# RMSNorm and matmul on one core: the loads of x move to ScalarE's DMA queue, in pieces of eight tiles

## The chip, the core and the metric

The kernel runs on one core of one Trainium2 chip. TensorE (PE), VectorE (DVE), ScalarE (ACT), GpSimd (POOL) and SyncE (SP) each run their own instruction list in order and wait for one another by semaphores. Transfers between HBM and the on-chip memory are issued by an engine (here SP, and ACT for one small one) and carried out by the core's 16 DMA engines. The metric is the device time of the core in microseconds (us), the median of several runs.

## The reference

```python
# x [16, 1024, 512] f32, gamma [512] f32, weight [512, 768] f32, eps
rms = np.sqrt(np.mean(x ** 2, axis=-1, keepdims=True) + eps)
x_norm = x / rms * gamma
return np.matmul(x_norm, weight).astype(np.float32)     # [16, 1024, 768]
```

## The kernel before

The 16,384 rows of x are 128 tiles of 128 rows. A tile of x is 256 KB of float32, a tile of the output 384 KB. Tiles go in pairs j = 0 to 63 (tiles 2j and 2j+1).

**The work on a tile.** gamma is folded into the weight once, at the start, and 1/rms is applied at the end, when the product leaves PSUM. So a tile goes through these steps: its rows are loaded into `xt` (line 176); ACT squares them and sums along the row (`square`, line 195); POOL casts them to bf16 (`cast`, line 187); PE transposes them as pairs of bf16 packed in a float32 word (`transpose_word`, line 229), and DVE copies the transposed tile back (`evac`, line 238); PE multiplies it by the weight in 8 matmuls (line 299) into one of three accumulators; ACT (even tiles, line 278) or DVE (odd tiles, line 280) scales the accumulator by 1/rms into `ot`; SP stores it (line 292). The last four tiles of every 16, from tile 16 on, are transposed by DVE in 32x32 blocks (line 270) after a POOL cast into `xq` (line 259).

**Buffers.** `xt` has two slots of 16 tiles, so tile i+32 overwrites tile i and may be loaded only when tile i has been cast and squared. `ot` has three slots of 8 tiles, so tile i+24 may be scaled only when the store of tile i's group has landed. PSUM has three accumulators, so tile i+3 may begin on PE only when tile i has been scaled.

**The order.** The class `Order` writes down every operation with what it reads and writes, in program order, and turns that into waits: each engine runs its own operations in the order written, and a transfer is issued by its engine at the place where it was written down. The main loop runs over the pairs. In the turn of pair j it writes down the casts, then the squares of the pair or pairs in `norm_turns` (pair j+4 for most of the run), then the matmuls of tiles 2j and 2j+1 with the transposes of pair j+2 between them, then the two scalings and the store, if the tile ends a group.

**The loads of x before the change.** All go out on SP, in the same list as the stores. Tiles 0 to 31 are loaded ahead of the loop, in pieces of 2, 2, 4, 8, 8 and 8 tiles, the first one before the two weight loads and the rest behind them. From there on, the loop calls

```python
        load_until((2 * j + AHEAD + XG - 1) // XG * XG)     # AHEAD = 20, XG = 16
```

at the head of each turn: groups of 16 tiles, as one load (tiles 32 to 79) or as two of 8 (from tile 80). SP issues in order, so a load that stands behind a store in SP's list is issued when that store's tiles have been scaled, and its data move behind that store's data. `rows` lays the tiles over the rows of x and out so that the bytes of one load or store lie together in each partition's stretch: a piece of 8 tiles is 16 KB of x, or 24 KB of the output, for each of 128 partitions.

Of the kernel before, what the change touches and what calls it, by code (L numbers as in the profile page):

```python
# [100 lines left out]
def kernel(  # L101
# [9 lines left out]
    PE, DVE, ACT, POOL, SP = nc.tensor, nc.vector, nc.scalar, nc.gpsimd, nc.sync  # L111
    order = Order(tc)
# [4 lines left out]
    x = x.flatten_outer_dims()  # L117
    out = out.flatten_outer_dims()
# [3 lines left out]
    NT = N // P  # L122
    NP = NT // 2
    XG, OG = 16, 8
    AHEAD = 20

    def stretches(group, parts):
        first, size, i = {}, {}, 0
        for g in range(NT // group):
            for n in parts.get(g, [group]):  # L130
                for t in range(i, i + n):
                    first[t], size[t] = i, n
                i += n
        return first, size

    last = NT // OG - 1
    x_first, x_size = stretches(XG, {0: [2, 2, 4, 8], **{g: [8, 8] for g in (1, 5, 6, 7)}})
    o_first, o_size = stretches(OG, {0: [1, 1, 2, 4], last - 1: [4, 4], last: [4, 2, 2]})

    def rows(ap, i, n):  # L140
        base, t = (x_first[i], x_size[i]) if i < XG else (i - i % XG, XG) if i < 2 * XG else (i - i % (2 * XG), 2 * XG)
        return ap[base * P:(base + t) * P, :].rearrange("(p t) d -> p t d", t=t)[:, i - base:i - base + n, :]

    def sb(name, shape, dtype):
# [26 lines left out]
    def x_of(i, n=1):  # L171
        return xt[i // XG % 2][:, i % XG:i % XG + n, :], cells("x", i // XG % 2, i % XG, n)

    def load(i):
        dst, to = x_of(i, x_size[i])
        order.transfer(SP, lambda: SP.dma_start(out=dst, in_=rows(x, i, x_size[i])), writes=to)  # L176

    starts = [i for i in range(NT) if x_first[i] == i]

    def load_until(i):  # L180
        while starts and starts[0] < i:
            load(starts.pop(0))

    def cast(i, n=1):
        src, of = x_of(i, n)
        s = i // 8 % 2
        run(POOL, lambda: POOL.tensor_copy(out=xb[s][:, i % 8:i % 8 + n, :], in_=src), of, cells("xb", s, i % 8, n))  # L187
# [3 lines left out]
    def square(i):  # L191
        src, of = x_of(i)
        j = squares[0] % 2
        squares[0] += 1
        run(ACT, lambda: ACT.activation(out=jk[j], in_=src[:, 0, :], func=AF.Square, accum_out=ssq[:, i:i + 1]),  # L195
            of, [("jk", j), ("ssq", i)])

    def root(i, n):
        s = slice(i, i + n)
        run(ACT, lambda: ACT.activation(out=rms[:, s], in_=ssq[:, s], func=AF.Sqrt, scale=1.0 / D, bias=eps_sb),  # L200
            [("ssq", t) for t in range(i, i + n)] + ["eps"], [("rms", i)])
        run(DVE, lambda: DVE.reciprocal(out=rstd[:, s], in_=rms[:, s]), [("rms", i)],  # L202
            [("rstd", t) for t in range(i, i + n)])

    def norms(i, n):
        for t in range(n):
            square(i + t)
        root(i, n)
# [6 lines left out]
    def norms_of_group(j):  # L215
        square(2 * j)
        square(2 * j + 1)
        if j in norm_end:
            root(*norm_end[j])
# [33 lines left out]
    def quad_of(j):  # L253
        return j // 2 if (2 * j) % XG >= XG - 4 and 2 * j >= XG else None

    def cast_quad(q):
        src, of = x_of(4 * q, 4)
        s = 4 * q // XG % 2
        run(POOL, lambda: POOL.tensor_copy(out=xq[s], in_=src), of, [("xq", s)])  # L259
        for t in range(4):  # L260
            xT_of[4 * q + t] = (xTq[s][:, t], ("xTq", s))
        words = xq[s].rearrange("p t d -> p (t d)").bitcast(F32).rearrange("p (a w) -> p a w", w=P)
        turned = xTq[s].rearrange("p t h m c -> p (t h m c)").bitcast(F32).rearrange("p (a m) -> p a m", m=P)
        for tokens in range(0, P, B):
            for features in range(0, P, B):
                quad_moves.append((turned[features:features + B, :, tokens:tokens + B],
                                   words[tokens:tokens + B, :, features:features + B], s))
# [4 lines left out]
    def move_quad(n):  # L272
        for _ in range(min(n, len(quad_moves))):
            move(*quad_moves.pop(0))
# [9 lines left out]
    def accumulator():  # L284
        return next(turns) % 3

    def store(i):
        first, n = o_first[i], o_size[i]
        s = first // OG % 3
        if i == first + n - 1:  # L290
            src = ot[s][:, first % OG:first % OG + n, :]
            order.transfer(SP, lambda: SP.dma_start(out=rows(out, first, n), in_=src), reads=cells("ot", s, first % OG, n))  # L292
# [12 lines left out]
    def matmuls(i, a, ks, feed=None):  # L305
        block, cell = xT_of[i]
        for k in ks:
            lhsT = block[:, k // 2, :, k % 2]
            hold(lhsT, cell)
            for half, lo, hi in ((0, 0, WIDE), (1, WIDE, O)):  # L310
                product(ops[a][:, lo:hi], lhsT, w_bf[:, k, lo:hi], k == 0, k == K - 1,
                        [cell, ("w", k, half)], [("ops", a, half)])
            if feed:
                feed()

    def finish_tile(i, a, engine):
        s = i // OG % 3

        before = [("ot", s, i % OG - 1)] if i == o_first[i] + o_size[i] - 1 else []
        scale(engine, ot[s][:, i % OG, :], ops[a][:, :O], rstd[:, i:i + 1],  # L320
              [("ops", a, 0), ("ops", a, 1), ("rstd", i)] + before, [("ot", s, i % OG)])
        store(i)

    def feeder(pairs, gaps, alone=False):
        queue = [(j, t, h) for j in pairs for t in range(2) for h in range(2)]
        calls = iter(gaps)

        def feed():
            for _ in range(next(calls)):
                j, t, h = queue.pop(0)  # L330
                transpose_word(j, t, h)
                if alone and h == 1:
                    evac(j, t, 1)
                elif (t, h) == (1, 1):
                    evac(j)
        return feed
# [6 lines left out]
    def load_weights(h):  # L343
        order.transfer(SP, lambda: SP.dma_start(out=w_f32[:, 2 * h:2 * h + 2, :].rearrange("p c o -> p (c o)"), in_=wv[:, h, :]),  # L344
                       writes=[("w_f", 2 * h), ("w_f", 2 * h + 1)])
# [1 line left out]
    load_until(2)  # L347
    load_weights(0)
    load_weights(1)
    load_until(2 * XG)  # L350

    run(DVE, lambda: DVE.memset(warm, 0.0), [], ["warm"])
    run(DVE, lambda: DVE.memset(eps_sb, float(eps)), [], ["eps"])  # L353
# [48 lines left out]
    mid, one, two, both = ([0, 0, 1, 1, 0, 1, 1, 0], [1, 1, 0, 1, 1, 0, 0, 0], [1, 0, 1, 0, 1, 0, 1, 0],  # L402
                           [1, 1, 1, 1, 1, 1, 1, 1])
    for j in range(1, NP):
        load_until((2 * j + AHEAD + XG - 1) // XG * XG)
        if j in (1, 2):
            cast(4 * j + 4, 4)
        elif j % 8 == 4 and j + 4 < NP:
            cast(2 * j + 8, 8)
        elif j % 8 == 6 and j + 2 < NP:  # L410
            cast(2 * j + 12, 4)
        if (2 * j + 2) % XG == 0 and 2 * j + 2 < NT:
            cast_quad((2 * j + 2 + XG - 4) // 4)
        elif 2 * j >= XG:
            move_quad(3)
        if j < 4:
            norms(2 * j + 2, 2)
        for pair in norm_turns.get(j, []):
            norms_of_group(pair)
        if j < 3:  # L420
            feed = feeder([j + 1], mid if j == 1 else one, alone=j == 1)
        elif j == 3:
            feed = feeder([4, 5], both)
        elif j + 2 < NP and quad_of(j + 2) is None:
            feed = feeder([j + 2], two)
        else:
            feed = None
        for i, engine in ((2 * j, ACT), (2 * j + 1, DVE)):
            a = accumulator()
            matmuls(i, a, range(K), feed)  # L430
            finish_tile(i, a, engine)
# [48 lines left out]
```

## Time and profile before

| what | value |
|---|---|
| runs | 208.95, 209.01, 209.52 us; median 209.01 us |
| the profiled execution's own time | 208.56 us |
| its span, first to last instruction | 206.8 us |
| PE busy | 192.9 us (93%) |
| DVE, ACT, POOL busy | 149.3, 144.5, 59.9 us |
| moved by DMA | 85.62 MB, mean 414 GB/s |
| read from and written to HBM | 35.13 MB and 50.33 MB |
| PE's last matmul ends | about 198.2 us |

The profiled execution took 1.8 us more than its span, and 0.45 us less than the median of the runs. Busy time is summed over the whole span and says little where two engines are near their limits at once; the rows by stretches of time say more. DMA shares are means over the 16 DMA engines.

### The profile page before, as it was taken

Reading aid. Unit: us, or ns where it says so; the run is one execution under the profiler, and the core shown is the slowest. Engines: PE = TensorE matmul, PEld = TensorE weight load, DVE = VectorE, ACT = ScalarE, POOL = GpSimd, SP = SyncE. Lnnn points to the kernel's source line nnn. Section 1 sums busy time; section 2 is a strip of 40 time slices with the busy share of each in tenths; the row PEclk is TensorE's granted clock in tenths of the full one; section 3 lists DMA queues with packets and bytes.
Section 4 is the critical chain, followed back from the end, with each engine's and each line's share of the span. In section 5 each row is a group of like instructions: output and inputs, shape, how many; then the busy total and the mean of one; then the engine's idle time right before and its main releaser. Section 6 shows DMA issues by size and latency. Waiting matters only on the chain.

```text
span 206.8 us, 2761 instructions
## 1 busy us (share of the span) xinstructions
PE 192.9 (93%) x1212; PEld 72.5 (35%) x717; DVE 149.3 (72%) x255; ACT 144.5 (70%) x343; POOL 59.9 (29%) x34
## 2 busy tenths in 40 slices
PE   7789999999999999998999999999999999999930
PEld 1234443432343333342333333433343333343300
DVE  0455647998589966998469984999569984999520
ACT  4798897868768496864977687677867787673310
POOL 2247651009300291004900660006700274000000
PEclk9999999999999999999999999999999999999996
DMA  6999999999999999999999999999999999999993
GB/s 225 423 445 428 387 385 444 456 396 428 428 445 425 417 426 455 425 409 433 431 415 436 428 445 403 439 417 447 418 441 414 437 433 441 418 442 409 414 415 141
DMA packets 5632, 85.62 MB, mean 414 GB/s; under 512 B 626, under 2 KB 628, under 8 KB 1780
## 3 DMA queue, kind: packets, MB, share of 16 engines
q1 hardware_dynamic: 5616, 85.46, 97.6%
q8 instruction: 7, 0.11, 0.2%
q14 instruction: 5, 0.04, 0.0%
q10 hardware_dynamic: 4, 0.00, 0.0%
HBM read 35.13 MB, written 50.33 MB: 413 GB/s over the span
## 4 chain that ended last, share of the span: by engine, by line
PE 71%; DMA 16%; DVE 5%; issue 2%; SPq 1%; ACT 1%; POOL 1%; ACTq 0%
PE ps L299 62%; DMA xt<-in_x_dram 16%; PE ps L229 8%; DVE ot L280 2%; DVE xTq L270 2%; DVE xT L238 1%; POOL xb L187 1%; ACT jk L195 0%; SPq L344 0%; SPq L176 0%; ACT ot L278 0%; SPq L292 0%; DVE rstd L202 0%; SPq L475 0%; ACTq L93 0%
## 5 line engine op out<-in xcount | busy, mean ns | idle before, releaser
L299 PE MATMUL ps<-w_bf,xT 128*128 128x256 bf16 (+1 forms) x783 | 144.9, 325 | 2.6 <-DVE w_bf L280 0.8
L278 ACT ACTIVATE ot<-ps,rstd 128x768 f32<-128x768 f32 x64 | 57.4, 897 | 42.3 <-PE ps L299 40.7
L195 ACT ACTIVATE jk<-xt 128x512 bf16<-128x512 f32 x128 | 78.8, 619 | 7.7 <-DMA xt<-in_x_dram 7.7
L187 POOL CAST xb<-xt 128x2048 bf16<-128x2048 f32 (+3 forms) x21 | 46.3, 2221 | 111.9 <-DMA xt<-in_x_dram 93.3
L280 DVE TENSOR_SCALAR ot<-ps,rstd 128x768 f32<-128x768 f32 x64 | 64.8, 1013 | 9.4 <-PE ps L299 8.7
L295 PEld LDWEIGHTS <-xT 128*128 128x128 bf16 x400 | 39.3, 98 | 60.2 <-issue 52.1
L229 PE MATMUL ps<-ident_f,xb 128*128 128x128 f32 x200 | 54.1, 274 | 0.9 <-POOL xb L187 0.9
L238 DVE COPY xT<-ps 128x1024 bf16<-128x1024 bf16 (+1 forms) x53 | 34.5, 653 | 24.0 <-PE ps L229 22.3
L270 DVE STREAM_TRANSPOSE xTq<-xq 32x256 f32<-32x256 f32 x112 | 48.7, 435 | 3.4
L229 PEld LDWEIGHTS ps<-ident_f,xb 128*128 128x128 f32 x200 | 28.2, 142 | 46.5 <-issue 42.7
L299 PE MATMUL ps<-w_bf,xTq 128*128 128x256 bf16 (+1 forms) x217 | 41.8, 324 | 0.4
L195 ACT ACTIVATION_READ_ACCUMULATOR jk<-xt 128x1 f32 x128 | 24.3, 190 | 0.0
L295 PEld LDWEIGHTS <-xTq 128*128 128x128 bf16 x112 | 11.0, 98 | 14.5 <-issue 14.5
L259 POOL CAST xq<-xt 128x2048 bf16<-128x2048 f32 x7 | 13.3, 1897 | 0.0
L202 DVE RECIPROCAL rstd<-rms 128x8 f32<-128x8 f32 (+3 forms) x20 | 3.9, 193 | 8.3 <-ACT rms L200 8.1
L200 ACT ACTIVATE rms<-ssq,eps_sb 128x8 f32<-128x8 f32 (+3 forms) x20 | 6.0, 300 | 0.7
L299 PE MATMUL ps<-warm 128*128 128x512 bf16 x10 | 4.4, 578 | 1.4 <-DVE eps_sb L353 1.4
L278 ACT ACTIVATE w_bf<-w_f,g_sb 128x768 bf16<-128x768 f32 x2 | 1.9, 936 | 1.1 <-DMA w_f<-in_weight_dram 1.1
L376 DVE COPY g_sb<-ps 128x4 f32<-128x4 f32 x1 | 0.2, 163 | 3.2 <-PE ps L370 3.2
L340 ACT ACT_TABLE_LOAD x1 | 1.3, 1283 | 1.5 <-SPq L434 1.5
L280 DVE TENSOR_SCALAR w_bf<-w_f,g_sb 128x512 bf16<-128x512 f32 (+2 forms) x3 | 1.4, 481 | 0.6 <-DMA w_f<-in_weight_dram 0.6
L370 PEld LDWEIGHTS ps<-ident_f,g_row 2*128 2x128 f32 x2 | 0.3, 202 | 2.6 <-issue 2.6
(10 smaller groups left out, 1.9 us busy)
## 6 DMA issues: line engine op xcount, KB each, us to landing
out_dram<-ot SPq DMA_DIRECT2D x13, 3072.0 KB, 16.5
xt<-in_x_dram SPq DMA_DIRECT2D x9, 2048.0 KB, 21.0
xt<-in_x_dram SPq DMA_DIRECT2D x3, 4096.0 KB, 22.7
out_dram<-ot SPq DMA_DIRECT2D x4, 1536.0 KB, 11.5
out_dram<-ot SPq DMA_DIRECT2D x3, 768.0 KB, 7.3
w_f<-in_weight_dram SPq DMA_DIRECT2D x2, 768.0 KB, 5.5
xt<-in_x_dram SPq DMA_DIRECT2D x2, 512.0 KB, 5.2
xt<-in_x_dram SPq DMA_DIRECT2D x1, 1024.0 KB, 9.0
```

Source lines behind the costliest of these rows:

```text
L187: run(POOL, lambda: POOL.tensor_copy(out=xb[s][:, i % 8:i % 8 + n, :], in_=src), of, cells("xb", s, i % 8, n))
L195: run(ACT, lambda: ACT.activation(out=jk[j], in_=src[:, 0, :], func=AF.Square, accum_out=ssq[:, i:i + 1]), of, [("jk", j), ("ssq", i)])
L200: run(ACT, lambda: ACT.activation(out=rms[:, s], in_=ssq[:, s], func=AF.Sqrt, scale=1.0 / D, bias=eps_sb), [("ssq", t) for t in range(i, i ...
L202: run(DVE, lambda: DVE.reciprocal(out=rstd[:, s], in_=rms[:, s]), [("rms", i)], [("rstd", t) for t in range(i, i + n)])
L229: run(PE, lambda: PE.transpose(out=tp[b][:, t, h, :], in_=words[:, lo:lo + P], identity=ident_f), cells("xb", s, j % 4 * 2 + t) + ["ident" ...
L238: run(DVE, lambda: DVE.tensor_copy(out=dst[:, t:t + n, :], in_=src[:, t:t + n, :]), [("tp", b)], cells("xT", j % 4, t, n))
L259: run(POOL, lambda: POOL.tensor_copy(out=xq[s], in_=src), of, [("xq", s)])
L270: run(DVE, lambda: DVE.transpose(out=dst, in_=src), [("xq", s)], [("xTq", s)])
L278: run(ACT, lambda: ACT.mul(out=dst, in_=src, mul=r), reads, writes)
L280: run(DVE, lambda: DVE.tensor_single_scalar(out=dst, in_=src, scalar=r, op=mybir.AluOpType.mult), reads, writes)
L295: run(PE, lambda: PE.ldweights(lhsT), [cell])
L299: run(PE, lambda: PE.add_instruction(mybir.InstMatmult(name=nc.get_next_instruction_name(), engine=mybir.EngineType.PE, ins=[PE.lower_ap(r ...
```

## The change

Three things are done. The pieces are 8 tiles throughout, so that tiles 32 to 79 are loaded in six pieces and not three. Loads of tiles 0 to 23 stay on SP ahead of the loop (`FIRST` = 24); all later loads are issued by ACT, so SP's list holds only stores from there on, and the first store stands right behind the load of tiles 16 to 23. And the places in the loop change: tiles 24 to 31 are loaded in the turn of pair 2, and from then on a piece of 8 in every fourth turn, beginning with tiles 32 to 39 in the turn of pair 5, each starting eleven pairs (`LEAD`) ahead. In ACT's list such a load stands behind the squares of its turn and ahead of the scaling of tile 2j. The layout of rows is the same as before for each tile. The instruction lists of PE, DVE and POOL are the same in both kernels; ACT's gains 13 DMA issues, and no wait; SP's loses 10 load issues.

```diff
-    AHEAD = 20
+    FIRST, LEAD = XG + OG, 11
...
-    x_first, x_size = stretches(XG, {0: [2, 2, 4, 8], **{g: [8, 8] for g in (1, 5, 6, 7)}})
+    x_first, x_size = stretches(OG, {0: [2, 2, 4]})
...
-        base, t = (x_first[i], x_size[i]) if i < XG else (i - i % XG, XG) if i < 2 * XG else (i - i % (2 * XG), 2 * XG)
+        base, t = (i - i % OG, OG) if OG <= i < XG else (x_first[i], x_size[i]) if i < OG else (i - i % XG, XG) if i < 2 * XG else (i - i % (2 * XG), 2 * XG)
...
         dst, to = x_of(i, x_size[i])
-        order.transfer(SP, lambda: SP.dma_start(out=dst, in_=rows(x, i, x_size[i])), writes=to)
+        queue = SP if i < FIRST else ACT
+        order.transfer(queue, lambda: queue.dma_start(out=dst, in_=rows(x, i, x_size[i])), writes=to)
...
-    load_until(2 * XG)
+    load_until(FIRST)
...
     for j in range(1, NP):
-        load_until((2 * j + AHEAD + XG - 1) // XG * XG)
...
         for pair in norm_turns.get(j, []):
             norms_of_group(pair)
+        if j == 2 or j > 2 and (j + LEAD) % 4 == 0:
+            load_until(2 * XG if j == 2 else 2 * (j + LEAD) + OG)
```

## The prediction

> **What bounds the kernel now.** I read the slices of the page first, then the queues, then busy time by stretches, then the waits and the timeline near a wait.
>
> ```profile
> PE   7789999999999999998999999999999999999930
> DMA  6999999999999999999999999999999999999993
> q1 hardware_dynamic: 5616, 85.46, 97.6%
> q8 instruction: 7, 0.11, 0.2%
> ```
>
> PE and the DMA engines are both full from the second slice to the end. q1 is SP's queue, with every load and store of the loop; q8 fetches instructions.
>
> ```profile
> 12.00:198.00 186.00, 183.71 (x1175) 69.92 (x694) 144.83 (x242) 137.12 (x329) 56.83 (x25) 1.00 1.00 426
> ...
> 21.00:24.00 3.00, 2.95 (x21) 1.26 (x13) 1.77 (x4) 2.31 (x7) 2.28 (x1) 1.00 1.01 421
> 24.00:27.00 3.00, 3.00 (x22) 1.22 (x12) 1.62 (x2) 3.00 (x10) 1.32 (x1) 1.00 0.93 287
> 42.00:45.00 3.00, 3.00 (x22) 1.18 (x13) 2.87 (x7) 2.08 (x6) 0.00 (x0) 1.00 0.94 374
> ...
> 198.00:201.00 3.00, 0.17 (x2) 0.00 (x0) 1.02 (x1) 0.00 (x0) 0.00 (x0) 1.00 0.97 406
> 201.00:204.00 3.00, 0.00 (x0) 0.00 (x0) 0.00 (x0) 0.00 (x0) 0.00 (x0) 0.89 0.72 299
> ```
>
> Columns: stretch, its length, busy PE, PEld, DVE, ACT, POOL, clock, DMA share, GB/s. The DMA share is 1.00 for 186 us at 426 GB/s: there is no gap to fill, in any stretch, only a rate. It drops at 24 to 27 (287) and at 42 to 45 (374). In the packet records of the trace a 16 KB packet takes 608 ns, a 24 KB one 912 and a 32 KB one 1,213, to the nanosecond, except in these stretches.
>
> How close is PE as a bound? The pairs repeat every 23.42 us for 16 tiles (SP's stores at 35.58 and 59.00). 16 tiles are 4.19 MB in and 6.29 MB out, so PE asks for 10.49 MB / 23.42 us = 448 GB/s. DMA gives 426. So DMA is the tighter of the two and a backlog grows.
>
> ```profile
> ACT jk L195 <- DMA xt<-in_x_dram: 7.7, 6, 3.0
> ...
> 95.65 0.63 ACT L195 ACTIVATE jk<-xt 128x512 bf16<-128x512 f32 x1 [3.03 <-DMA xt<-in_x_dram]
> 97.82 1.46 PE L299 MATMUL ps<-w_bf,xT 128*128 128x512 bf16 x8 [0.72 <-ACT ot L278]
> ```
>
> That backlog reaches PE once: tiles 64 to 79 come late, ACT's square waits 3.03 us, and PE 0.72. At the end, PE finishes at 198.2, DVE scales to 199.2, and the last store (768 KB) is issued at 199.5 and lands after 6.3, at 205.8. The first load finds an empty queue: 512 KB in 3.4 us, the least of all loads, of which 1.2 are data at 426. So 768 KB would take 1.8 + 2.2 = 4.0, and the end has some 2.3 us of backlog in it.
>
> **The change part by part.** I sum against the profiled span, 206.8; its execution took 208.56, 0.45 below the median.
>
> Bytes: the same. Packets: six pieces of 16 KB rows for three of 32 KB, 48 packets of 608 ns on each engine for 24 of 1,213, so +0.07 us.
>
> The slow stretches: (426 - 287) x 3 / 426 = 0.98 us, and (426 - 374) x 3 / 426 = 0.37. Both lie where all 16 engines finish a load with stores next. By the packet records the load packets there run long (850 to 1,190 ns for 608 at 24 to 27) and the stores do not; the later such places cost 0.15 us falling to 0.03, as the engines drift apart. From store to load nothing is lost. After the change the load of tiles 24 to 31 runs beside the first stores instead of ahead of them, so I count the 0.98 as gone. Bounds: 0, if it moves to wherever stores first start; -1.5, if all six places go. I take -1.0.
>
> Two queues on each engine: this is the cost that the trace doesn't show. Most of the time an engine now has load packets of one queue and store packets of the other before it. The 13 loads from ACT make 13 x 8 = 104 visits to the second queue on each engine. Bound above: the only second queue here, q8, needs 940 ns for its 16 KB packets (608 on q1), and the packet behind it is 360 to 470 long, so 0.34 + 0.36 = 0.7 us a visit, or 73 us. Bound below: on one queue, store to load costs 0, and load to store on engines that are out of step mostly 0. I take 0: q8's packets come alone to a sleeping queue, while here both are full, as the loads and stores are in the drifted stretches, which hold 426. A gain can't be excluded, but 426 against 431 (16 KB in 608 ns, 16 engines) leaves 2 us at most.
>
> The Trainium skill speaks against this change. "DMA: Bandwidth & Descriptors", "Rules for kernel authors", says that spreading transfers over queues brings no bandwidth, since they interleave on the same engines; the share of 1.00 agrees that there is none to be had. The same page, "Latency and other measured facts", gives copies over both queues 207 to 214 GB/s in each direction; as an estimate of mine, 414 in all would make 186 us at 426 some 5 us longer, and 428 one us shorter. No run here shows either.
>
> ACT's 13 issues: an issue of x takes SP 0.34 to 1.04 us, so 4.4 to 13.5 us of ACT's list. ACT waits 40.7 us for PE ahead of its scalings (L278), 0.92 in most pairs, and a scaling may be 1.6 us late (two tiles of 1.3 us on the other accumulators, less 0.90 for the scaling) before PE waits. So 0; without that cover, up to 13.5. The slots that the loads overwrite have been cast and squared several pairs earlier.
>
> The later loads: issued every 11.7 us; alternating with stores one takes 8 x (0.608 + 0.912) = 12.2 us, so the lag grows 0.5 a load, from 13.5 us to 19. The squares of these tiles come seven pairs after the issue, 20.5 us, with 1.6 of slack. They hold, and the 0.72 of PE goes. The margin at the last load is 3 us.
>
> The early loads: here the change costs something. By the GB/s of the stretches, the data of tile 23 end at 20.7 (cast at 21.72). Now ACT issues tiles 24 to 31 after its root at 15.9, data from about 17.4, and shares the engines with tiles 16 to 23, of which 3.2 us are left: they end at 23.8, are seen at 24.8, and the cast of 3.60 us ends at 28.4. PE's first transpose of tile 16 is at 28.31. PE waits 0.1 to 1.1 us; I take 0.3. Stores: the first start behind tile 23, 2 us earlier; their slots are due at 47.7, far away.
>
> PE's end is then 198.2 - 0.72 + 0.3 = 197.8, and with 2.3 us of backlog behind it a DMA saving of 1.0 reaches the end whole. Sum: 206.8 + 0.07 - 1.0 + 0 = 205.9 span, 207.65 execution, 208.1 in the median. Where this stall goes, the next to be late is again the data of the last stores.
>
> **The rivals.** *No change*, 209.0: the slow stretch comes back where stores start, and the total stays bytes over rate. For it: the share of 1.00. Against: nothing of the old hand-over is left.
>
> *All of it*, 206.1: six hand-overs gone (-1.5), and the engines, whose last packets end between 202.4 and 205.4 in the packet records, evener, so that no backlog is left: PE's end at 197.5, 1.3 to the last issue, 4.0 to land, 1.0 to the end, 203.8 of span. For it: it needs no more than the bounds above. Against: it needs a rate near 431 for 186 us.
>
> *Slower, by the switch between queues*: it cancels the gain at 1.0 us / 104 = 10 ns a visit and is slower by over 0.3% from 16 ns. At 50 ns, a small part of q8's 700 and about what a late hand-over costs, it is 5.2 - 1.0 = +4.2: 213.2. For it: every visit of q8 or q14 to an engine costs, and PE already asks for more than DMA gives. Against: both queues are never empty.
>
> That loads don't move to the second queue is excluded by the instruction lists.
>
> **How the numbers follow.** About 0.3% (0.63 us) is what a measurement of this kernel can tell from no change. Forecast 208.1, chance 0.35, own range 207.2 to 208.4. All of it, 0.10. No change, within 0.63, 0.15. Slower by the switch, 0.32; slower because PE waits early or ACT's issues run long (+1 to +2), 0.08. So faster 0.45, same 0.15, slower 0.40. The range reaches from the second case, less the 0.3% of a measurement, 205.5, to 50 ns a visit, 213.2; dearer switches are left out.
>
> **What would show it.** Right: 24 to 27 us above 400 GB/s, a second queue with about 27 MB, packets still at 608 and 912 ns, no wait of ACT near 95, PE's end near 197.8, DMA full to about 203. Wrong: load packets beside stores well over 608 ns and GB/s between 40 and 160 under 420; or PE waiting for the cast of tile 16 for over 2 us; or ACT's scalings waiting behind DMA issues.

## The result, and the profile after

The changed kernel takes 214.41 us in the median of 20 runs (209.17 to 219.45), the kernel before 209.0 us in 20 runs beside them (208.61 to 209.52): 2.6% slower, and above the predicted range, which ended at 213.2. The ratio is 1.0061, 95% interval [1.0038, 1.0084], if runs over 1.5% above a kernel's fastest are left out, as 13 of this kernel's 20 are; the kernel before has no such run, and the second and third profiles below show what goes with that scatter. Its profiled execution took 213.27 us, with a span of 211.4 at a mean granted TensorE clock of 0.996.

From the page of the changed kernel, the rows that answer to those of before (busy tenths in 40 slices; packets, MB and share of 16 engines for each queue):

```profile
PE   7789999999999999999999999999997989979890
DMA  6999999999999999999999999999999999887597
q1 hardware_dynamic: 4176, 58.20, 65.4%
q10 hardware_dynamic: 1876, 27.27, 30.7%
```

The second queue carries its 27 MB, as forecast. DMA, full up to the last slice before, now has holes in the last six. Busy time by stretches of the changed kernel, with the columns as before (stretch, length, PE, PEld, DVE, ACT, POOL, clock, DMA share, GB/s):

```profile
12.00:198.00 186.00, 180.63 (x1155) 67.84 (x673) 141.11 (x237) 135.16 (x327) 57.13 (x25) 1.00 0.98 413
...
24.00:27.00 3.00, 3.00 (x22) 1.18 (x13) 1.65 (x3) 3.00 (x8) 3.00 (x1) 1.00 0.98 310
42.00:45.00 3.00, 3.00 (x22) 1.22 (x12) 2.88 (x6) 2.12 (x5) 1.86 (x1) 1.00 1.02 437
...
189.00:192.00 3.00, 3.00 (x20) 1.22 (x12) 2.87 (x5) 0.90 (x1) 0.00 (x0) 1.00 0.38 164
195.00:198.00 3.00, 2.58 (x17) 0.69 (x8) 2.84 (x5) 0.90 (x1) 0.00 (x0) 1.00 0.23 94
```

The stretch at 24 to 27 us is slow still (310 for 287 GB/s, so 0.82 us is lost there for 0.98). At 42 to 45 the rate is back. Near 190 the loads are done, and PE is too late to give DMA stores: DMA works for 0.38 and 0.23 of the time. PE's last matmul ends at 205.9, 7.7 us later than before. What made PE late, from the waits of the changed kernel (us in total, times, longest):

```profile
DVE xTq L271 <- POOL xq L260: 10.2, 5, 3.2
...
ACT jk L196 <- DMA xt<-in_x_dram: 4.5, 5, 1.6
PE ps L300 <- DVE ot L281: 4.3, 6, 1.5
```

The first row is new: DVE's block transposes (the last four tiles of each 16) wait for POOL's cast of them. These casts, and not the squares, meet the late load first. One such place in the changed kernel's timeline (start, duration, engine, line; the idle time before it in brackets):

```profile
155.01 1.90 POOL L188 CAST xb<-xt 128x2048 bf16<-128x2048 f32 x1 [9.62 <-DMA xt<-in_x_dram]
156.85 1.90 POOL L260 CAST xq<-xt 128x2048 bf16<-128x2048 f32 x1
...
158.78 1.37 DVE L271 STREAM_TRANSPOSE xTq<-xq 32x256 f32<-32x256 f32 x3 [2.83 <-POOL xq L260]
...
161.85 0.48 PE L300 MATMUL ps<-w_bf,xT 128*128 128x512 bf16 x2 [1.15 <-DVE ot L281]
```

Read it downwards: the piece of tiles 104 to 111, issued at 131.57, is whole at 154.9. POOL casts four tiles for PE and then four for DVE, DVE starts 2.83 us late, its scaling of an odd tile behind that is late too, and PE waits 1.15 for the accumulator. Without the wait DVE would have begun at 155.95, so the piece was due at 155.95 - 3.74 = 152.2. On the median of the 16 engines it had landed at 150.1; the last engine came at 154.9. The squares of these tiles waited too, but only 0.92 us, from 154.05 on.

The packet records give a ledger. "Nominal" is all packets at their undisturbed times (611, 912 and 1,213 ns for 16, 24 and 32 KB, 460 for 12 KB), "excess" what they took above, "idle" the time without packets before and after 198 us, all in us per engine. "Spread" is the longest time between the first and the last of 16 engines in the landing of one transfer, "long stores" the 24 KB packets over 50 ns above nominal between 30 and 180 us. With the first packet at 2.0 us and up to 1 us of other queues' packets, which are left out here, a row adds up to the end of the data within 1.3 us, since neighbouring packets overlap a little. The profiled executions:

| kernel | us | nominal | excess | idle < 198 | idle > 198 | data end | PE end | spread | long stores |
|---|---|---|---|---|---|---|---|---|---|
| before | 208.56 | 199.0 | 2.4 | 0.2 | 1.9 | 205.4 | 198.2 | 3.8 | 14 |
| after | 213.27 | 199.2 | 3.4 | 5.0 | 0.8 | 210.1 | 205.9 | 9.1 | 128 |
| after, second (e9) | 209.65 | 199.2 | 3.0 | 2.1 | 0.4 | 206.4 | 202.1 | 5.0 | 74 |
| after, third (e10) | 219.17 | 199.2 | 6.8 | 5.9 | 2.2 | 215.8 | 211.6 | 12.3 | 130 |
| e1, one queue | 209.59 | 199.2 | 3.9 | 1.3 | 0.3 | 206.4 | 202.2 | 3.3 | 7 |
| e2, fifteen ahead | 209.54 | 199.2 | 2.8 | 0.9 | 1.6 | 206.2 | 200.3 | 5.0 | 53 |
| e11, both | 209.56 | 199.2 | 3.6 | 0.1 | 1.8 | 206.3 | 198.8 | 3.6 | 8 |
| e13, seventeen ahead | 210.67 | 199.2 | 3.7 | 1.6 | 1.1 | 207.3 | 202.3 | 9.5 | 119 |
| e5, stores in fours | 209.79 | 200.0 | 3.2 | 0.1 | 1.7 | 206.6 | 197.7 | 8.8 | |
| e6, fours, fifteen ahead | 209.67 | 200.0 | 3.0 | 0.3 | 1.5 | 206.2 | 200.1 | 7.0 | |
| e7, before, stores in fours | 211.28 | 199.8 | 3.7 | 1.8 | 1.4 | 208.1 | 203.1 | 4.6 | |
| e8, x in sixteens | 210.91 | 198.8 | 2.2 | 4.1 | 0.9 | 207.8 | 203.4 | 5.9 | 11 |
| e14, tiles 24 to 31 alone | 209.24 | 199.0 | 3.0 | 0.0 | 2.3 | 206.1 | 197.9 | 4.1 | 13 |
| e3, transfers, two queues | 206.03 | 199.2 | 1.3 | 0.1 | 1.2 | 202.9 | | 3.1 | 5 |
| e4, transfers, one queue | 210.05 | 199.2 | 4.8 | 0.1 | 1.7 | 206.9 | | 2.9 | 0 |

So the 4.7 us of the profiled execution are, to within 0.2, idle DMA before 198 us (+4.8) and excess (+1.0), less 1.1 of idle time after it.

### The profile page after: what moved, and what is told of

The parts are those of the page before. It is cut to its first block, busy times and chain, and to the rows that moved or that the text cites. A ratio compares the mean times of both kernels' runs of the same rounds, so it can differ in the third digit from the quotient of the medians.

```text
span 211.4 us, 2794 instructions
## 1 busy us (share of the span) xinstructions
PE 197.1 (93%) x1236; PEld 72.3 (34%) x717; DVE 149.8 (71%) x255; ACT 145.1 (69%) x343; POOL 60.0 (28%) x34
## 4 chain that ended last, share of the span: by engine, by line
PE 39%; DMA 37%; DVE 13%; POOL 4%; issue 3%; SPq 1%; ACT 0%; POOLq 0%; ACTq 0%
DMA xt<-in_x_dram 37%; PE ps L300 34%; DVE xTq L271 5%; DVE ot L281 5%; PE ps L230 5%; DVE xT L239 2%; POOL xb L188 2%; POOL xq L260 2%; ACT jk L196 0%; SPq L345 0%; SPq L177 0%; DVE rstd L203 0%; ACT ot L279 0%; POOLq L93 0%; SPq L477 0%
## 5 line engine op out<-in xcount | busy, mean ns | idle before, releaser
L300 PE MATMUL ps<-w_bf,xT 128*128 128x512 bf16 (+1 forms) x800 | 149.8, 326 | 5.5 <-DVE ot L281 4.3
L271 DVE STREAM_TRANSPOSE xTq<-xq 32x256 f32<-32x256 f32 x112 | 48.8, 436 | 13.6 <-POOL xq L260 10.2
L300 PE MATMUL ps<-w_bf,xTq 128*128 128x512 bf16 x224 | 42.8, 326 | 0.8 <-DVE xTq L271 0.8
```

Of the source, the lines that this page charges most:

```text
L271: run(DVE, lambda: DVE.transpose(out=dst, in_=src), [("xq", s)], [("xTq", s)])
L300: run(PE, lambda: PE.add_instruction(mybir.InstMatmult(name=nc.get_next_instruction_name(), engine=mybir.EngineType.PE, ins=[PE.lower_ap(r ...
```

## The experiments

**The queue and the lead (e1, e2, e11).** Three kernels that keep all else of the change.

```diff
 e1:   queue = SP                            # for SP if i < FIRST else ACT
 e2:   FIRST, LEAD = XG + OG, 15             # for 11
 e11:  both
```

> The changed kernel with one thing undone: all loads are issued by SP, at the same places of the program. Theory A (one of the 16 DMA engines falls into a slow alternation between the two queues: in the changed kernel's profile its 24 KB store packets take 912 + about 140 ns from 90 us on, and every load and store waits for that engine): with one queue there is no alternation, 24 KB packets stay at 912 ns on every engine, the spread of the 16 landings of a load stays under 4 us, and the runs lie together within 1 us, at 208.0 to 209.5. Theory B (no engine is slow; the loads only come too late, because alternating packets give them 16 of 40 KB, and pieces of 8 tiles issued eleven pairs ahead are too late in any case): in one queue a load stands behind one store at most, so B also expects 208 to 210, and PE's waits gone; B alone expects nothing of the scatter. Theory C (the pieces of eight and the later places cost, whatever the queue): 211 or more.

> The changed kernel with loads from tile 32 on fifteen pairs ahead for eleven, both queues kept: each load is issued 11.7 us earlier. Theory A: the slow engine still moves its bytes late, so runs still scatter over several us and the median stays above 211; PE's waits for loads shrink, so some us less than 214.4 are possible, but not the 209.0 of before. Theory B: the lateness is at most 8 us, 11.7 us more of lead takes all of it away: 207.5 to 209.0 in every run, no scatter.

> All loads on SyncE's queue, with the new pieces, fifteen pairs ahead and not eleven. Theory S: on one queue the loads move in the order of issue, so the lead is worth what the late block transposes cost with eleven pairs (4.5 us at PE's end, 202.2 against 197.7): PE ends by 199, the time is that of the transfers, and those need 206.9 to 207.3 us of span as on one queue without computing plus its own end: 209 to 209.8, against 210.6 with eleven pairs. Theory C (the pieces of eight and their hand-overs cost, wherever they stand): 210.5 or more, with an excess of the packets over their nominal times of 3.9 us or more.

| median, us | one queue | two queues |
|---|---|---|
| eleven pairs ahead | 210.63 (209.59 to 210.85), ratio 1.0059 [1.0037, 1.008] | 214.41 (209.17 to 219.45) |
| fifteen pairs ahead | 209.97 (209.56 to 211.03), ratio 1.0052 [1.0032, 1.0072] | 210.14 (209.25 to 211.58), ratio 1.0052 [1.0028, 1.0076] |
| transfers alone (e3, e4) | 210.34 | 206.14 |

Neither part is at fault by itself. In the medians the second queue costs 3.8 us with eleven pairs and nothing that can be seen with fifteen; the shorter lead costs 0.7 on one queue and 4.3 on two. With eleven pairs the quickest runs on one and on two queues are alike (209.59 and 209.17), so what the second queue adds is the scatter. With four pairs more, the waits of DVE for POOL's cast fall from 10.2 us to 2.8 on two queues, and on one from 6.9 to 1.5 (from the waits of e1, e2 and e11):

```profile
DVE xTq L271 <- POOL xq L260: 6.9, 6, 1.5
```

```profile
DVE xTq L271 <- POOL xq L260: 2.8, 2, 1.9
```

```profile
DVE xTq L271 <- POOL xq L260: 1.5, 1, 1.5
```

What is left in e11, with PE's end at 198.8 and next to no idle DMA, is the excess of 3.6 us for 2.4 before; that it comes from the greater number of hand-overs between loads and stores is argued, not shown. e11 lay above its "209 to 209.8" by 0.2. e1 lay above what theories A and B expected and just under C's 211, and e2 between A's 211 and B's 209.0, so none of the three is the whole account.

**The transfers by themselves (e3, e4).** `run` adds nothing to the order, so that only the DMAs remain.

```diff
     def run(engine, issue, reads=(), writes=()):
-        order.add(1, engine, issue, reads, writes)
+        pass                                # and three memsets of ot
 e4 also:  queue = SP
```

> Only the transfers of the changed kernel, on its two queues, with all computing left out (the output buffers are set to zero once, and each transfer goes as soon as its queue reaches it). Theory A: the alternation by itself makes slow engines: in some runs several us more than the one-queue twin, runs scattered by 2 us or more, and an engine with 24 KB packets at about 1,050 ns for tens of us. Theory B: no loss: 85.5 MB at 426 to 431 GB/s, a span of 201 to 205 us, the same as the one-queue twin within 1 us and with as little scatter. If the slow alternation needs the computing (its traffic in the on-chip memory), this kernel shows none.

> The twin: the same transfers, all on SP's queue, computing left out. Both theories: a span of 201 to 205 us, packets at 608 and 912 ns, runs within 0.5 us. It also says whether the slow stretch at 24 to 27 us (287 GB/s in the kernel before, 310 in the changed one) belongs to the transfers: if it does, it is here too; if it belongs to the computing, the rate stays above 420 there.

206.14 (206.03 to 206.8) and 210.34 (210.05 to 210.67). By stretches, first e3, then e4 (stretch, length, busy DVE and POOL, clock, DMA share, GB/s):

```profile
18.00:21.00 3.00, 0.00 (x0) 0.00 (x0) 1.00 1.00 426
24.00:27.00 3.00, 0.00 (x0) 0.00 (x0) 1.00 1.01 431
30.00:198.00 168.00, 0.00 (x0) 0.00 (x0) 1.00 1.01 429
```

```profile
18.00:21.00 3.00, 0.00 (x0) 0.00 (x0) 1.00 1.08 328
21.00:24.00 3.00, 0.00 (x0) 0.00 (x0) 1.00 0.88 351
24.00:27.00 3.00, 0.00 (x0) 0.00 (x0) 1.00 1.12 474
27.00:30.00 3.00, 0.00 (x0) 0.00 (x0) 1.00 1.00 328
30.00:198.00 168.00, 0.00 (x0) 0.00 (x0) 1.00 1.00 425
```

So alternating between queues is not dear: it is cheaper by 4.2 us than one queue with the same pieces, of which 3.5 are excess (4.8 and 1.3). I had expected the two within 1 us of each other and a span of at most 205 us, where e4's is 208.3. The slow stretch is there without any computing in e4, and twice, from 18 us and from 27 us on: by the packet records, at the end of the loads of tiles 16 to 23 and of tiles 24 to 31. In e3 the load packets of 18 to 30 us take 612 to 616 ns in the mean, and there is no such stretch. Against the excess of the kernel before (2.4) that is 1.1 us, about the gain predicted, but the transfers of the kernel before were not run by themselves. With the computing the excess is 3.0 to 6.8.

**The early part alone (e14).** In the kernel before, only tiles 24 to 31 go to ACT's queue in the turn of pair 2.

```diff
-    load_until(2 * XG)
+    load_until(XG + OG)
+        queue = ACT if XG + OG <= i < 2 * XG else SP
+        if j == 2:
+            load_until(2 * XG)              # the loop's own loads from j = 3 on
```

> The kernel before with one part of the change alone: tiles 24 to 31 are loaded by ScalarE in the turn of pair 2, with the first stores right behind tile 23 on SyncE's queue; all later loads as before, on SyncE's queue. The prediction's step (the slow stretch of 0.98 us goes when the load runs beside the first stores): 24 to 27 us above 400 GB/s, 207.9 to 208.4. The bound it left out (the slow stretch is where the small first stores start, wherever that is): a stretch under 360 GB/s within 21 to 30 us, 208.7 to 209.3. Other side: nothing here should slow the later part; over 209.7 would mean that the earlier stores or the later load of tiles 24 to 31 cost by themselves.

208.91 (208.59 to 209.24), ratio 1.000 [0.999, 1.0011]. The stretch and the wait of ACT near 95 us are both still there, from its rows by stretches and its timeline:

```profile
24.00:27.00 3.00, 3.00 (x22) 1.22 (x12) 1.62 (x2) 3.00 (x10) 3.00 (x1) 1.00 0.99 313
```

```profile
95.37 0.63 ACT L196 ACTIVATE jk<-xt 128x512 bf16<-128x512 f32 x1 [2.71 <-DMA xt<-in_x_dram]
```

So the term is 0 and not -1.0. But the small stores do not bring the stretch, as the bound had it. In e14 the load's 16 KB packets run beside the first small stores from 22.8 us on; up to 24 us they take 656 ns in the mean, from 24 us on 852 (623 and 850 in the changed kernel). In the kernel before, the same load's last packets take 890 to 980 from 24.2 us on, and the first store's data begin only at 26.3. So the stretch is the last third of the load of tiles 24 to 31, on either queue. Not every load ends like this: that of tiles 32 to 39 in the changed kernel ends near 37 us with packets of 611 ns. Why those of tiles 24 to 31 are long stays open.

**The changed kernel again, twice (e9, e10).** No edit.

> The changed kernel once more, for a second profile of it. Its runs lie between 209.2 and 219.5, so something in one execution decides. Theory A (one of the 16 DMA engines moves its 24 KB store packets some 140 ns slower, and the loads' landings wait for it): the time goes with the spread of the landings of one load over the engines; a run near 209.2 has a spread under 4 us at 180 us and no packet of 24 KB over 1,000 ns beyond a few dozen, a run of 213 or more has a spread of 8 us or more and 100 or more such packets. Theory S (the loads get 16 of every 40 KB while both queues are full, and the last four tiles of a group come late for POOL's cast whatever the engines do): the waits of DVE's block transposes for POOL's cast are 3 us or more in sum in a fast run too, the second halves of each 16 tiles take 13.4 us or more, and the spread does not tell a fast run from a slow one.

> The changed kernel a third time, for a third profile; the theories expect what they expect of the second. Together with the profile at hand, three points of time against spread, slow packets and PE's waits: theory A expects the three in one order, theory S the same waits in all three.

209.65 and 219.17 us: by chance one near each end of the scatter. The same waits, first of the quicker (e9), then of the slower one (e10):

```profile
DVE xTq L271 <- POOL xq L260: 6.6, 5, 1.8
...
ACT jk L196 <- DMA xt<-in_x_dram: 2.0, 2, 1.6
PE ps L300 <- DVE ot L281: 1.9, 6, 0.4
```

```profile
DVE xTq L271 <- POOL xq L260: 14.7, 5, 4.8
ACT jk L196 <- DMA xt<-in_x_dram: 11.2, 7, 2.9
...
PE ps L300 <- DVE ot L281: 8.4, 5, 3.0
```

Time, waits and spread go in one order over the three profiles (209.65, 213.27, 219.17 us; 6.6, 10.2, 14.7; 5.0, 9.1, 12.3). Both theories have a share. The late casts are there in the quick run too, as theory S said. How much they cost goes with lagging DMA engines, as theory A said, though not with one alone: of e10's load of tiles 104 to 111, issued at 136.1, 14 of 16 parts had landed by 152.4 us and the last two came at 162.5. The packet records do not name the engine; followed from end to start, an estimate, one engine of e10 needs some 1,050 ns for a 24 KB store in the mean of 60 to 120 us, and a second some 1,010. Theory S's "the same waits in all three" fell, and theory A's "under 4" for a quick run was 5.0. Three profiles are few; the order is shown, not a law.

Part of e10's time is not the DMA's. Twice PE waits 3.0 us, and less than 1 us after each wait the granted clock drops to 0.5 for 3.4 us. From the timeline of e10, then from its rows by stretches:

```profile
114.70 0.48 PE L300 MATMUL ps<-w_bf,xT 128*128 128x512 bf16 x2 [3.02 <-DVE ot L281]
...
169.51 0.49 PE L300 MATMUL ps<-w_bf,xT 128*128 128x512 bf16 x2 [3.03 <-DVE ot L281]
```

```profile
115.00:120.00 5.00, 5.00 (x24) 1.77 (x14) 4.74 (x11) 2.12 (x5) 0.00 (x0) 0.66 0.99 419
...
170.00:175.00 5.00, 5.00 (x24) 1.79 (x13) 4.77 (x10) 2.12 (x5) 0.18 (x1) 0.66 1.08 465
```

At half speed 3.4 us lose 1.7 each time, an estimate: 3.4 of the 9.5 us between e9 and e10. e8 has one such wait, of 3.1 us, and a clock of 0.57 from 136 to 140 us. After waits of at most 1.7 us (e10 and the other two profiles) the clock stays at 1.00. So a late load that holds PE up for 3 us costs more than the wait.

**Seventeen pairs ahead (e12, e13).**

```diff
 e12:  FIRST, LEAD = XG + OG, 17
 e13:  the same, but
-        if j == 2 or j > 2 and (j + LEAD) % 4 == 0:
-            load_until(2 * XG if j == 2 else 2 * (j + LEAD) + OG)
+        if j in (2, 5) or j > 5 and (j + LEAD) % 4 == 0:
+            load_until(2 * XG if j == 2 else 3 * XG if j == 5 else 2 * (j + LEAD) + OG)
```

> Two queues, seventeen pairs ahead and not eleven, which is the most that two slots of 16 tiles allow. The loads find their slots free only just. Theory S: with fifteen pairs the waits for late tiles were already small (2.8 us of DVE's, 0.9 us of idle DMA); seventeen take those too, and the end is set by the transfers: 208.5 to 209.5, PE's end near 198. Theory A: a slow engine still makes the last landings late, the time stays where fifteen pairs put it, 209.2 to 211.6 with a median near 210. Other side: ACT's issue waits for POOL's casts to free the slot, PE waits for ACT's scalings behind it, 211 or more.

> Two queues, seventeen pairs ahead, but tiles 32 to 47 are loaded in the turn of pair 5 (in the run with seventeen pairs from the start, tiles 40 to 47 stood ahead of the squares of tiles 12 to 15 in the order written, which then waited for them and squared their data: 17.6 us of PE's time). Theory S with a slow engine on top (an engine that is some 9% behind makes the landings late by up to 10 us, and the lead decides whether that reaches PE): with some 9 us more lead than eleven pairs nothing waits for a load: PE's end near 198, no scatter, all runs within 1.5 us, and the data end at 2.0 + 199.2 + some 3 of excess + 1 of other queues + 1 idle = 206.2, so 208.5 to 210. Theory A alone (the slow engine itself sets the end): scatter as with eleven pairs, 209 to 215. Other side: ACT's issues wait for POOL or for squares, PE behind it: 211 or more.

e12 took 224.24 us (223.72 to 224.95), and its timeline shows one wait that accounts for it, the squares behind a load that was written down too early; PE waits 17.6 us behind it:

```profile
41.93 0.63 ACT L196 ACTIVATE jk<-xt 128x512 bf16<-128x512 f32 x1 [19.75 <-DMA xt<-in_x_dram]
```

So e12 says nothing of the lead. e13 took 210.69 (208.99 to 212.63), ratio 1.0057 [1.0034, 1.008]; I had expected 208.5 to 210 without scatter. In its profile the landings of the loads are spread again (9.5). The lead keeps the scatter smaller (3.6 us for 10.3), but now the stores come late, whose slots ACT needs; from e13's waits:

```profile
ACT ot L279 <- DMA out_dram<-ot: 10.3, 5, 2.5
...
DVE xTq L271 <- POOL xq L260: 6.0, 3, 2.3
```

These stores are not held back by a lagging engine: those issued from 82 to 144 us spread by 3 to 4 us only, but land 21 to 24 us after their issue on the median engine, for 17 to 19 in the changed kernel.

**Other shares of the queues (e5, e6, e7, e8).** If each queue sends one packet in turn, the loads' share is set by the packets: 16 of every 40 KB. e5 to e7 halve the store packets, e8 doubles the load packets.

```diff
 e5:  o_first, o_size = stretches(OG, {**{g: [4, 4] for g in range(last)}, 0: [1, 1, 2, 4], last: [4, 2, 2]})
 e6:  the same, with LEAD 15;   e7: the same stores in the kernel before
 e8:  x_first, x_size = stretches(XG, {0: [2, 2, 4, 8], 1: [8, 8]})
      if j in (2, 5) or j > 3 and j % 8 == 3:
          load_until(2 * XG if j == 2 else 3 * XG if j == 5 else 2 * j + 42)
```

> The changed kernel with one thing changed: the stores go out in fours (12 KB packets) for eights (24 KB). Theory S (share): with both queues full an engine takes one packet of each in turn, so loads get 16 of 40 KB, 171 GB/s of 427, where PE uses 179; the load queue is never empty from 51 us on and falls behind by 0.7 us a piece, the quad tiles' cast on POOL and DVE's block transposes wait, PE waits, and at the end the stores run dry and the DMA engines stand idle. Here loads get 16 of 28 KB, 244 GB/s: a piece takes 8 x (0.611 + 0.466) = 8.6 us for 12.4, is read in time, DVE's wait for POOL's xq (10.2 us) and the DMA's idle time before 198 us (5 us) go, and so does the scatter: 206.5 to 208.5. Theory A (one engine in a slow alternation): packets still alternate, more often even, so runs still scatter over several us with a median above 211.

> As e5, and loads fifteen pairs ahead. Theory S: with 244 GB/s the loads are no longer late with eleven pairs, so the four pairs more add little: 206 to 208.5, within 0.7 of e5; a little less if one slow engine still makes a load late now and then. Theory A: as e5.

> The kernel before with its stores in fours: the control for e5. On one queue the packets of loads and stores don't alternate, so the size of a store changes no share. Theory S: no gain, within 0.7 us of 209.0 (12 KB packets cost 466 for 456 ns, some 0.7 us over the run, and the store of four lands earlier). If fours by themselves are worth something, e.g. at the end or by an earlier store, it shows here.

> The changed kernel with loads from tile 32 on in pieces of 16 tiles (32 KB packets) on ACT's queue, issued where the whole slot has been cast and squared (turns 5, 11, 19, 27 and so on); stores in eights. Theory S: loads get 32 of 56 KB, 57%, as in e5, by another edit, and half as many visits to the second queue: a load of 16 takes 17 us, is there 26 us before its last reader, so no waits: 206.5 to 208.5, the same as e5 within 0.7. The other side: stores get 43% while a load runs, and if a store lands later than its slot is needed (23 us after its issue), PE waits there: then 209 or more.

Measured: e5 210.96 (ratio 1.0079 [1.0058, 1.01]), e6 209.74 (1.0034 [1.0022, 1.0046]), e7 211.19 (1.0091 [1.0061, 1.0122]), e8 211.1 (1.0069 [1.0035, 1.0103]). Theory S's times for e5, e6 and e8 (206 to 208.5) were all missed. e5 does to the engines what the share says: no wait of DVE for POOL's cast is left, PE ends at 197.7, no DMA is idle. It is 3.5 us quicker than the changed kernel, but not than the one before: the stores in fours cost by themselves, 2.2 us in e7, where I had expected at most 0.7 (ACT's squares wait 15.9 us for loads there, 7.7 before), and e5's data still end at 206.6. In e6 and e8 the stores are what comes late, here from e6's waits and then e8's:

```profile
ACT ot L279 <- DMA out_dram<-ot: 20.4, 8, 3.7
```

```profile
ACT ot L279 <- DMA out_dram<-ot: 10.2, 2, 6.1
DVE ot L281 <- DMA out_dram<-ot: 4.6, 2, 3.3
PE ps L300 <- ACT ot L279: 4.3, 2, 3.1
```

With the share moved to the loads, the stores miss their slots. This fits the reading that DMA has no share to give away, as PE asks for more than DMA moves.

**What makes an engine lag (e15 to e18).** The transfers of e3, with some of the work put back.

```diff
 e15: square, cast and cast_quad are added to the order again (ACT, POOL)
 e16: the scalings are (ACT, DVE), of a constant tile, into ot
 e17: both;   e18: both, with queue = SP
```

> The transfers of the changed kernel on two queues, with the squares on ACT and the casts on POOL, nothing else; the outputs are zeros. What makes one engine's store packets slow (over 50 ns above 912, between 30 and 180 us: 5 in the transfers alone, 74 to 130 in the changed kernel)? If it is on-chip memory read by other engines while loads write it: 40 or more such packets. If not: under 20, and about 206 us.

> The transfers of the changed kernel on two queues, with 128 scalings on ACT and DVE, of a constant, that write the buffers that the stores read, nothing else; the outputs are ones. If the writing beside the stores' reading makes the slow packets: 40 or more over 50 ns. If it is only that stores then come when a tile is ready: a few. About 206 us without.

> Squares, casts and the scalings of a constant beside the transfers on two queues, no PE and no other work of DVE; the outputs are ones. If on-chip memory traffic of ACT, POOL and DVE makes an engine slow: 40 or more slow store packets and a spread of the landings over 4 us. If it needs PE, DVE's block transposes or the pace that PE gives the stores: under 20 and a spread under 4, about 206 to 207 us.

> The same work with all loads on SyncE's queue; the outputs are ones. Store packets at 912 ns (under 20 slow ones) as in all kernels with one queue; load packets with the hand-overs' excess, 10 to 25 ns in the mean against 3 to 8 on two queues; about 210 us, 3 to 4 more than on two queues.

206.21, 205.74, 206.4 and 210.24 us, with 5, 9, 3 and 1 long stores and spreads of at most 2.4, 1.9, 2.3 and 4.1 us. In these runs, one each, reading x and writing the output buffers beside the transfers makes no engine lag, and the 4 us between one queue and two stay. That points at what is left out here: PE, the PSUM reads, DVE's transposes and the pace that PE gives the stores. It does not show it, as two queues and all the computing do not always bring long stores either: e8 has 11 and e12 20. The cause stays open.

## Why the prediction was wrong

**The step that failed: "They hold, and the 0.72 of PE goes".** It had two errors. The due time was taken from the squares, 20.5 us behind the issue with 1.6 of slack; the first reader of a group's last four tiles that matters is POOL's cast for DVE's block transposes, which the prediction named nowhere. For tiles 104 to 111 that reader was due 20.6 us after the issue, the squares 22.5. The larger error was that the lag, "from 13.5 us to 19", was that of a mean engine. As such it was right: on the median engine the pieces of tiles 72, 88, 104 and 120 landed 18.3, 18.7, 18.5 and 18.0 us after their issue. But the reader waits for the last of 16 engines, and that came after 21.5, 22.2, 23.3 and 24.8. The step had also been warned: it put a piece at 12.2 us against a period of 11.7, so the load queue could only fall behind until 3 us were left of the margin, and it had counted with no engine behind the others. The price was PE's end, 197.8 forecast and 205.9 measured (202.1 in the quick run). That the pieces were late is shown by the waits, and by the lead that takes them away; why engines lag so far on two queues is not known.

**The -1.0 us of the slow stretch.** Failed. Its bound of 0 is what e14 shows (ratio 1.000), though not for the reason given with it, "if it moves to wherever stores first start": the stretch stayed with the end of the load, now beside stores (852 ns a packet). e4 shows such stretches in transfers without computing. Giving up the gain would have led to 209.0, the first rival, and still not to 214.

**The switch between queues, taken as 0.** Right on most engines: beside each other the packets take 611 and 912 ns, as before the change. The prediction's 608 was misread: of the 1,152 packets of 16 KB in the kernel before, 823 take 611 ns and none less than 608. (With 611 the smaller pieces cost 0.2 us and not 0.07, as in the ledger, and the full rate is 429 and not 431.) In e3 the two queues even save 4.2 us against e4, more than "2 us at most". Wrong for the engines that lag, the slowest of which takes some 50 to 140 ns longer for a store in the mean (60 to 120 us of the three profiles, the same estimate as for e10). The rival "slower by the switch" priced a cost on all engines that adds to the end; what came was a cost on one or two engines that became waits of PE, so that its 213.2 lies near the 214.4 by luck. On the Trainium skill: "DMA: Bandwidth & Descriptors", "Rules for kernel authors", has it that spreading over queues brings no bandwidth. From 30 to 198 us that agrees (429 and 425 GB/s in e3 and e4); at the hand-overs e3 gains what the rule does not speak of. The same page's 207 to 214 GB/s in each direction, which it gives for copies at two row pitches (at others 97 to 164), would make 414 to 428 in all, an estimate; the 429 of e3 stand at its upper end.

**What held.** Bytes and packets. ACT's 13 issues took 0.33 to 0.37 us each, and nothing waited for them. The early loads were forecast to cost PE 0.3 us and cost nothing: tiles 16 to 23 landed at 23.5 us (24.8 forecast), their cast ended at 27.2, and PE's first transpose of them, at 28.5, did not wait. PE does run 0.2 us later there, but it has done so from the first tiles on, before ACT issues its first load at 16.1: the stores of tiles 4 to 7, 8 to 15 and 16 to 23 were issued at 24.0, 35.8 and 48.3 us, before at 23.8, 35.6 and 48.1. The observation that DMA is the tighter bound held too, but DMA time in which PE gives it no store was not priced: 5.0 us of idle before 198 us. Two sums of the prediction are 0.1 off and change nothing: two tiles of 1.3 us less 0.90 are 1.7 and not 1.6, and a span of 203.8 makes 206.0 and not 206.1.

## What to carry to other kernels

Before moving loads to another queue, list every first reader of each tile, not only the one that the loop names, and set its due time against the landing on the last engine, with the share of the queue that the packet sizes give (16 of 40 KB here) as its rate. Where DMA is full, lateness is dealt out: in e6, e8 and e13 what the loads gained the stores lost. So look to the lead before the queue: fifteen pairs for eleven took 4.3 us off the median on two queues, though no kernel here with these pieces came under the time before. And look at several runs of a kernel: one of 209.65 and one of 219.17 us were the same program.

## What the runs showed of the hardware that was not expected

Two queues with full lists take turns packet by packet: from 42 to 45 us of the changed kernel 32 store packets of 24 KB and 32 load packets of 16 KB start, and in e3 from 33 to 36 us 64 store packets of 3 KB and 64 load packets. In the transfers alone this is almost free (excess 1.3 us in all), while the same transfers on one queue have 4.8. The slow stretch is the end of an early load, with or without stores beside it: at 24 to 27 us (287, 310 and 313 GB/s), or from 18 and from 27 us on (328 both times, e4). 12 KB store packets took 463 to 465 ns in the mean (e5 to e7) for half of 912; that is some 1 us of e7's 2.2, and more idle DMA (1.8 us for 0.2) goes with the rest. One or two DMA engines of 16 fell up to 12 us behind the others (e10), for a reason that is open. And in e10, after PE had stood still for 3.0 us, TensorE's granted clock was 0.5 for 3.4 us.
